# Three of four down batches in seven half-size products, one weight sum made by an accumulating DMA, and an eviction product by product

## The chip, the cores and the metric

The kernel runs on one core of a Trainium2 chip. The metric is device time of one execution in microseconds, the median of several runs.

## What is computed

Two layers of a decoder trunk, 256 tokens of width 2048, float32. Layer 0 mixes tokens by differential attention, layer 1 by a gated recurrence; each is followed by the MLP, the only part that the change touches, and by a gated embedding ("PLE") of the side input p.

```python
def sqrelu_mlp(xn, w_up, w_down):
    return jnp.square(jax.nn.relu(xn @ w_up)) @ w_down

    for i in range(DEPTH):
        ...
        h = h + sqrelu_mlp(rmsnorm(h, g_mlp[i]), w_up[i], w_down[i])
        ...
```

w_up[i] is 2048 x 8192 and w_down[i] 8192 x 2048. The output is the residual stream h (256 x 2048).

## The kernel before

**Float32 on TensorE.** Each float32 operand is split into a high part hi, rounded to TensorE's float32r, and lo = src − hi. ScalarE copies hi (`split`, L356; `split_form`, L464) and VectorE subtracts (L357; L471). A product is then three matmuls: hi·hi, lo·hi and hi·lo, in a seven or plain group in the order of L518, L519 and L521. All weights go through this: a chunk of 512 rows x 512 columns (1 MB) is loaded by SyncE's queue (`load_to`, L457), and a "sub", half of it (256 rows, so 128 partitions x 1024 elements), is split for one step of matmuls.

**Order of the work.** `stream` walks over groups; in each sub it first loads up to two chunks ahead (W_RAW − 1), then splits up to three subs ahead (W_SPLIT − 1), and then writes the sub's matmuls. A scheduler may reorder across engines, so the program's order alone does not fix that of an engine. Raw chunks rotate over three buffers `w_raw` and, every fourth, one in the pool `big`. In the MLP hi/lo pairs rotate over six places: four in the pool `wsp`, one pair of `v4` buffers, one `big` (`split_to`, L481).

**The MLP.** The hidden width is cut into 16 batches of 512. `up(b)` multiplies the weights of batch b by all tokens (8 subs of 16 matmuls, L537), and `up_evict` squares the relu and splits the result. Two ups are followed by a `down` group, over 1024 of the 2048 output columns (`half` 0 or 1) and mostly four batches; per layer: half 1 with batches {0, 1} (the first group), then in turn half 0 and half 1 with {0..3}, {2..5}, {4..7}, ... {12..15}, and at the end half 1 with {14, 15}. So a layer has six full groups, three of each half, one first group of two batches, and the last two groups stand back to back, six batches long.

**Seven products.** A batch of a down group is a 2 x 2 block problem: tokens in two halves, the 512 rows by the parity of their 128-row block, 1024 columns in two chunks. A plain batch takes the eight block products (4 subs of 12 matmuls). A seven batch takes Strassen's seven in Winograd's form (7 subs of 6 matmuls): `FORMS` lists for each its weight operand, its hidden operand and its product P1 to P7, and `SUMS` the weight operands that are sums of blocks (W11, W21 the two row parities of chunk 0, W12, W22 of chunk 1), made by VectorE (L470) one sub ahead. The hidden operand's sums are made in `up_evict` (L810, L814, L815), for j in two halves, so that an up's eviction for a seven batch splits 896 columns where a plain one splits 512. Even batches are seven, odd ones plain (`is_seven`). So the batches of a full group are seven, plain, seven, plain.

**Accumulators and eviction.** All batches of a group add into the same PSUM accumulators, one for each product. P3 and Z (the second token half and chunk of the plain batches) come from the pool `tp`, the others from `acc`. When P1, P5, P6 and P7 are all complete `middle` combines them (one ScalarE copy, L836, L837, twice L839), and at the group's end `evict` adds eight parts to the residual h (L848). At a layer's last groups h goes on to the next norm (`feed`), whose transposes are deferred by one or two subs.

Of the kernel before, what the change touches and what calls it, by code (L numbers as in the profile page):

```python
# [17 lines left out]
P = 128  # L18
# [43 lines left out]
class Group:  # L62
# [41 lines left out]
class Blocks:  # L104


    def __init__(self, w, b, n0):
        r0 = b * BT * P
        rows = w[r0 : r0 + BT * P].rearrange("(c p) n -> p c n", p=P)
        self.chunks = [Chunk(rows[:, :, n0 + i * NB : n0 + (i + 1) * NB], BT) for i in range(2)]  # L110
        for c in self.chunks:
            c.ring = 1
        self.sums = {}

    def of(self, name):
        if name in self.sums:
            return self.sums[name]
        return self.chunks[int(name[2]) - 1].raw[:, int(name[1]) - 1 :: 2]


class SevenGroup:
# [4 lines left out]
    def __init__(self, w, batches, n0, hid, middle, evict):  # L126
        self.hid, self.middle, self.evict, self.subs, self.pre = hid, middle, evict, [], {}
        self.what = []
        for b, seven in batches:
            bl = Blocks(w, b, n0)  # L130
# [11 lines left out]
        self.first, self.last = {}, {}  # L142
        for i, (_, form, nj) in enumerate(self.what):
# [3 lines left out]
        self.mid = max(self.last[k] for k in ("P1", "P5", "P6", "P7"))  # L147
# [27 lines left out]
def trunk_kernel(ctx: ExitStack, tc, a, out):  # L175
# [215 lines left out]
    class Norm(Wide):  # L391
# [35 lines left out]
        def feed(self, nb):  # L427
            self.stat(nb)
            for b in range(2):
                defer(1 + b, lambda b=b: self.transpose(nb, b))  # L430


    def stream(groups):
# [9 lines left out]
        def load_to(i):  # L443
            while done["load"] < min(i + 1, len(chunks)):
# [722 lines left out]
```

## Time and profile before

| | |
|---|---|
| median of 3 runs | 2303.68 us (2303.24 to 2303.95) |
| profiled execution | 2303.79 us, of which the trace spans 2301.9 |
| TensorE (PE) | busy 2277.8 us, 11275 matmuls |
| VectorE (DVE) | busy 1709.6 us, 74% |
| ScalarE (ACT) | busy 1355.5 us, 59% |
| GpSimd (POOL) | busy 47.3 us, 2% |
| mean granted TensorE clock | 1.00 |
| moved by the DMA engines | 434.8 MB, mean 189 GB/s |

Busy time counts stretches in which the engine executes something. Operations of one engine overlap a little, so the mean time of one is somewhat longer than the distance between starts. A line such as L357 is the source line in the kernel before; the line of a helper serves many callers. In the rows `t`, `big`, `v`, `x`, `w_hi`, `w_lo` and `w_raw` are buffers of the pools of those names, `acc` and `tp` PSUM accumulators, and an arrow stands for "written from".

### The profile page before, as it was taken

The page shows a single profiled execution, that of the slowest core. Times are in us where ns is not written, and L with a number is a line of the kernel's source. Part 1 is how long each engine was busy: PE and PEld are TensorE (multiplying, and loading weights), DVE is VectorE, ACT ScalarE, POOL GpSimd, SP SyncE. Part 2 cuts the span into 40 slices and gives each one's busy share as a digit, 9 for nine tenths or more (in the row PEclk, how much of TensorE's full clock was granted, in tenths as well). Part 3 has the DMA queues.
Part 4 walks back from the last instruction along what each step waited for, and adds up shares of the span by engine and source line. Part 5 has one row for each costly group of instructions (what it writes and reads, how often), then busy time and mean ns, then how long its engine had stood idle before and what let it go on. Part 6 is the DMA issues. An engine that isn't in the chain of part 4 may idle for free. (4 is left out here: it accounts for less than half of the span.)

```text
span 2301.9 us, 29004 instructions
## 1 busy us (share of the span) xinstructions
PE 2277.8 (99%) x11275; PEld 1913.4 (83%) x11275; DVE 1709.6 (74%) x2048; ACT 1355.5 (59%) x1836; POOL 47.3 (2%) x79
## 2 busy tenths in 40 slices
PE   8999999999999999999999999999999999999999
PEld 7888888888888888887888887888888888888787
DVE  6676655778878868879666767568887887887974
ACT  6555555655655645646557887555564564564653
POOL 2100000000000000000000000000000000000000
PEclk9999999999999999999999999999999999999999
DMA  7455556456547547545555565645745645745464
GB/s 244 165 185 168 165 171 214 168 182 237 181 162 242 187 161 244 175 162 186 193 190 190 165 201 173 202 157 200 256 151 179 238 167 181 239 167 179 174 210 146
DMA packets 221050, 434.80 MB, mean 189 GB/s; under 512 B 7326, under 2 KB 12064, under 8 KB 220912
## 3 DMA queue, kind: packets, MB, share of 16 engines
q1 hardware_dynamic: 220256, 432.04, 55.5%
q8 instruction: 88, 1.44, 0.3%
q0 software_dynamic: 608, 0.89, 0.2%
q14 instruction: 50, 0.41, 0.1%
q10 hardware_dynamic: 48, 0.02, 0.0%
HBM read 430.82 MB, written 2.10 MB: 188 GB/s over the span
## 5 line engine op out<-in xcount | busy, mean ns | idle before, releaser
L357 DVE TENSOR_TENSOR w_lo<-w_raw,w_hi 128x1024 fp32r<-128x1024 f32 x465 | 564.2, 1221 | 304.5 <-ACT w_hi L356 304.4
L356 ACT CAST w_hi<-w_raw 128x1024 fp32r<-128x1024 f32 x465 | 486.6, 1051 | 419.4 <-PE acc L352 214.9
L537 PE MATMUL acc<-x,w_hi 128*128 128x512 f32 x1368 | 477.3, 396 | 0.0
L350 PE MATMUL acc<-w_hi,x 128*128 128x512 f32 x1152 | 457.1, 397 | 0.0
L351 PE MATMUL acc<-w_lo,x 128*128 128x512 f32 x1152 | 450.4, 391 | 1.9 <-DVE w_lo L357 1.9
L352 PE MATMUL acc<-w_hi,x 128*128 128x512 f32 x1152 | 450.6, 391 | 0.0
L537 PE MATMUL acc<-x,w_lo 128*128 128x256 f32 x1368 | 368.5, 279 | 0.0
L537 PEld LDWEIGHTS acc<-x,w_hi 128*128 128x128 f32 x1368 | 251.9, 188 | 54.7
L537 PEld LDWEIGHTS acc<-x,w_lo 128*128 128x128 f32 x1368 | 257.8, 188 | 7.4
L352 PEld LDWEIGHTS acc<-w_hi,x 128*128 128x128 f32 x1152 | 216.7, 188 | 46.7 <-DVE x L357 0.2
L351 PEld LDWEIGHTS acc<-w_lo,x 128*128 128x128 f32 x1152 | 217.2, 189 | 44.9 <-DVE w_lo L357 3.1
L350 PEld LDWEIGHTS acc<-w_hi,x 128*128 128x128 f32 x1152 | 216.8, 188 | 41.7
L464 ACT CAST w_hi<-t 128x1024 fp32r<-128x1024 f32 x85 | 89.2, 1051 | 128.8 <-PE acc L537 73.9
L537 PE MATMUL acc<-x,big 128*128 128x512 f32 (+1 forms) x688 | 127.7, 338 | 0.0
L356 ACT CAST w_hi<-big 128x1024 fp32r<-128x1024 f32 x87 | 90.7, 1050 | 62.6 <-PE acc L537 26.7
L471 DVE TENSOR_TENSOR w_lo<-t,w_hi 128x1024 fp32r<-128x1024 f32 x85 | 103.8, 1222 | 30.3 <-ACT w_hi L464 30.1
L537 PE MATMUL acc<-x,v 128*128 128x512 f32 (+1 forms) x672 | 124.8, 338 | 0.0
L537 PEld LDWEIGHTS acc<-x,big 128*128 128x128 f32 x688 | 107.9, 188 | 15.5
L537 PEld LDWEIGHTS acc<-x,v 128*128 128x128 f32 x672 | 105.9, 188 | 15.0
L357 DVE TENSOR_TENSOR w_lo<-big,w_hi 128x1024 fp32r<-128x1024 f32 x87 | 105.3, 1218 | 14.1 <-ACT w_hi L356 14.1
L471 DVE TENSOR_TENSOR w_lo<-w_raw,w_hi 128x1024 fp32r<-128x1024 f32 x64 | 78.0, 1219 | 31.9 <-ACT w_hi L464 31.9
L518 PE MATMUL acc<-w_hi,x 128*128 128x512 f32 x256 | 100.3, 392 | 1.4 <-ACT w_hi L464 1.3
(277 smaller groups left out, 3570.0 us busy)
## 6 DMA issues: line engine op xcount, KB each, us to landing
w_raw<-in_w_up_dram SPq DMA_DIRECT2D x96, 1024.0 KB, 5.5
w_raw<-in_w_down_dram SPq DMA_DIRECT2D x96, 1024.0 KB, 5.2
w_raw<-in_w_qkv_dram SPq DMA_DIRECT2D x47, 1024.0 KB, 5.1
big<-in_w_up_dram SPq DMA_DIRECT2D x32, 1024.0 KB, 5.6
big<-in_w_down_dram SPq DMA_DIRECT2D x32, 1024.0 KB, 7.3
w_raw<-in_w_ple_gate_dram SPq DMA_DIRECT2D x32, 1024.0 KB, 5.2
w_raw<-in_w_in_rec_dram SPq DMA_DIRECT2D x32, 1024.0 KB, 5.4
w_raw<-in_w_o_attn_dram SPq DMA_DIRECT2D x16, 1024.0 KB, 5.1
```

Of the source, the lines that this page charges most:

```text
L350: nc.tensor.matmul(ps, lhsT=lh, rhs=rh, start=start, stop=False)
L351: nc.tensor.matmul(ps, lhsT=lh, rhs=rl, start=False, stop=False)
L352: nc.tensor.matmul(ps, lhsT=ll, rhs=rh, start=False, stop=stop)
L356: nc.scalar.copy(hi, src)
L357: nc.vector.tensor_tensor(lo, src, hi.bitcast(F32), op=ALU.subtract)
L464: nc.scalar.copy(s.hi, src)
L471: nc.vector.tensor_tensor(s.lo, src, s.hi.bitcast(F32), op=ALU.subtract)
L518: nc.tensor.matmul(acc[k], lhsT=lh, rhs=rh, start=first, stop=False)
L537: nc.tensor.matmul(o, lhsT=lh, rhs=rh, start=k == 0 and n == 0, stop=k == g.nk - 1 and n == 1)
```

## The change

- Batch b is plain only if b mod 4 is 1. Full groups of half 0 are then seven, plain, seven, seven; those of half 1 seven, seven, seven, plain; the last two groups seven, plain, seven, seven and seven, seven.
- U1 = W11 + W12 is made by a DMA from GpSimd's queue that adds the first half of chunk 0, read once more from DRAM, onto the first half of chunk 1 in SBUF, so W12 alone is no longer there; the other three sums stay on VectorE, T3 in another form. A seven batch's chunks are loaded in two pieces, one for each row parity.
- The products come in another order, P1, P2, P3 first, and each is handed to `done` in the sub after which it is complete: P2, P4, P3 and Z are added to h at once, the combination of P1, P6, P7, P5 as it becomes possible. P4, and P7 where the group has a plain batch, now come from `tp`.
- To make room: the hi/lo places fall from six to five; a fourth buffer of the size of a weight sum (`t4`); batch 3, 7, 11 and 15 keep their operands in two `big` buffers; the transposed p moves to a `big` buffer and is made at the end of each MLP instead of earlier, and the next norm's transposes are deferred further.

In the changed kernel the lines are: lo splits L367 and L482, hi copies L366 and L476, sums L481, loads L467, the accumulate L469, the up's eviction L819 to L828, the combination L862, L867, L871, adds to h L847.

```diff
-    ("W11", X11, "P1"), ("U1", S1, "P5"), ("T2", S2, "P6"), ("T3", S3, "P7"), ("W21", X12, "P2"),
-    ("T4", X22, "P4"), ("W22", S4, "P3"),
+    ("W11", X11, "P1"), ("W21", X12, "P2"), ("W22", S4, "P3"), ("U1", S1, "P5"), ("T2", S2, "P6"),
+    ("T3", S3, "P7"), ("T4", X22, "P4"),
 )
-SUMS = {"U1": ("W11", "W12"), "T2": ("U1", "W22"), "T4": ("T2", "W21"), "T3": ("W12", "W22")}
+SUMS = {"T2": ("U1", "W22", ALU.add), "T3": ("T2", "W11", ALU.subtract), "T4": ("T2", "W21", ALU.add)}
...
-        self.chunks = [Chunk(rows[:, :, n0 + i * NB : n0 + (i + 1) * NB], BT) for i in range(2)]
-        for c in self.chunks:
+        cols = [rows[:, :, n0 + i * NB : n0 + (i + 1) * NB] for i in range(2)]
+        self.chunks = [Chunk(c, BT) for c in cols]
+        for i, c in enumerate(self.chunks):
             c.ring = 1
+            if seven:
+                half = lambda raw, i: raw[:, i * SK : (i + 1) * SK]
+                c.pieces = [(lambda raw, i=i: half(raw, i), cols[c is self.chunks[1]][:, i::2]) for i in range(2)]
+        if seven:
+            self.chunks[1].more = (lambda raw: raw[:, :SK], cols[0][:, 0::2])
...
+        self.aside = ("P4", "P7") if len(self.subs) % len(FORMS) else ("P4",)
...
-        return wk.tile(shape, dtype, tag="t4", name="t4", bufs=3)
+        return wk.tile(shape, dtype, tag="t4", name="t4", bufs=4)
...
+                if c.more is not None:
+                    nc.gpsimd.dma_start(c.more[0](c.raw), c.more[1], accum_op=ALU.add)
...
-                    at = turn["split"] % (W_SPLIT + 2) if s.chunk.ring else 2
-                    if at == 0:
+                    if s.chunk.ring and turn["split"] % (W_SPLIT + 1) == 0:
                         s.hi, s.lo = (v4([P, SK, NB], F32R) for _ in range(2))
-                    elif at == 1:
-                        both = big([P, 2, SK, NB], F32R)
-                        s.hi, s.lo = both[:, 0], both[:, 1]
...
-                    if i == g.mid:
-                        g.middle(acc)
+                    for k in acc:
+                        if g.last[k] == i:
+                            g.done(k, acc)
...
+    ALONE = {"P2": (0, 0), "P4": (1, 0), "P3": (0, 1), "Z": (1, 1)}
...
-        return b % 2 == 0
+        return b % SLOTS != 1
...
+            if at == 3:
+                return Batch(True, big([P, 2, 7, P], F32R), big([P, 2, 7, P], F32R))
...
+            def done(k, acc):
+
+                have.add(k)
+                if k in ALONE:
+                    add(*ALONE[k], acc[k])
+                if k == "P1":
+                    c1 = t4([P, 2, NB])
+                    keep["P1"], keep["M"] = c1[:, 0], c1[:, 1]
+                    nc.scalar.copy(keep["P1"], acc["P1"])
+                if "A" not in have and {"P1", "P6"} <= have:
+                    have.add("A")
+                    nc.vector.tensor_tensor(keep["M"], keep["P1"], acc["P6"], op=ALU.subtract)
...
             def evict(acc):
...
+                for q, at in (("P1", (0, 0)), ("B", (1, 0)), ("M", (0, 1)), ("N", (1, 1))):
+                    add(*at, keep[q])
                 if bs[-1] == NBT - 1:
                     for n in range(2):
-                        norm_out().feed(2 * half + n)
+                        norm_out().feed(2 * half + n, 2 + 2 * n if half else 4 + 3 * n)
+                    if half == 0:
+                        defer(7, lambda: p_setup(l))
```

Three places show how the order of the instructions moves. The first is VectorE's queue at the start of a full group of half 0 (batches 4 to 7), around the up's eviction (`t_4401` and `t_4412`, with the change `t_5874` and `t_5888`, are the halves of the hidden operand). Before:

```order
L471 TENSOR_TENSOR w_lo<-t_4381,w_hi 128x1024
L471 TENSOR_TENSOR v_4439<-w_raw,v_4438 128x1024
L806 TENSOR_TENSOR t_4401<-acc,t_4402 128x2x128
L806 TENSOR_TENSOR t_4401<-acc,t_4405 128x256
L806 TENSOR_TENSOR t_4412<-acc,t_4413 128x2x128
L806 TENSOR_TENSOR t_4412<-acc,t_4416 128x256
L357 TENSOR_TENSOR big<-t_4401,big 128x512
L357 TENSOR_TENSOR big<-t_4412,big 128x512
L471 TENSOR_TENSOR big<-t_4441,big 128x1024
L471 TENSOR_TENSOR w_lo<-w_raw,w_hi 128x1024
L357 TENSOR_TENSOR w_lo<-w_raw,w_hi 128x1024 x2
L357 TENSOR_TENSOR w_lo<-big,w_hi 128x1024
```

and with the change:

```order
L481 TENSOR_TENSOR t_5920<-t_5907,w_raw 128x1024
L827 TENSOR_TENSOR t_5874<-t_5874 128x128
L823 TENSOR_TENSOR t_5888<-t_5888 128x256
L828 TENSOR_TENSOR t_5874<-t_5874 128x128
L827 TENSOR_TENSOR t_5888<-t_5888 128x128
L482 TENSOR_TENSOR v_5918<-t_5907,v_5917 128x1024
L367 TENSOR_TENSOR big<-t_5874,big 128x896
L828 TENSOR_TENSOR t_5888<-t_5888 128x128
L481 TENSOR_TENSOR t_5935<-t_5907,w_raw 128x1024
L367 TENSOR_TENSOR big<-t_5888,big 128x896
L482 TENSOR_TENSOR w_lo<-t_5920,w_hi 128x1024
L482 TENSOR_TENSOR w_lo<-t_5935,w_hi 128x1024
```

The four adds of the up (L806) were followed by two 512-column splits and the remaining lo splits of the first subs. Now the four adds (L819), the sum T2 (`t_5907`) and one of the hidden operand's sums stand just ahead of the rows shown; the sums T3 (`t_5920`) and T4 (`t_5935`), the hidden operand's other sums and two 896-column splits follow, with T2's lo (`v_5918`) among them, and the lo splits of T3 and T4 come last.

The second is SyncE's queue of loads around the group of half 1 with batches 2 to 5, with the numbers of the buffers. Before:

```order
L457 DMA w_raw_5135<-in_w_down_dram 128x4x512
L457 DMA w_raw_5216<-in_w_down_dram 128x4x512
L457 DMA big_5147<-in_w_down_dram 128x4x512
L457 DMA w_raw_5237<-in_w_down_dram 128x4x512
L457 DMA w_raw_5291<-in_w_down_dram 128x4x512
L457 DMA big_5303<-in_w_down_dram 128x4x512
```

and with the change:

```order
L467 DMA w_raw_5160<-in_w_down_dram 128x2x512 x2
L467 DMA w_raw_5250<-in_w_down_dram 128x2x512 x2
L467 DMA w_raw_5277<-in_w_down_dram 128x2x512 x2
L467 DMA big_5189<-in_w_down_dram 128x2x512 x2
L467 DMA big_5361<-in_w_down_dram 128x4x512
L467 DMA w_raw_5333<-in_w_down_dram 128x4x512
```

`big_5189` is the second chunk of the group's second batch (the numbers give the order in which buffers were asked for): it stands behind `w_raw_5250` and `w_raw_5277`, both chunks of the third. GpSimd's queue has its three accumulates of this group onto `w_raw_5093`, `w_raw_5277` and `big_5189`, in this order.

The third is VectorE's queue at the end of the group of half 0. Before:

```order
L357 TENSOR_TENSOR v_4680<-w_raw,v_4679 128x1024
L357 TENSOR_TENSOR big<-w_raw,big 128x1024
L357 TENSOR_TENSOR w_lo<-w_raw,w_hi 128x1024
L848 SCALAR_TENSOR_TENSOR h<-acc,n_r_3440,h 128x512 x2
L848 SCALAR_TENSOR_TENSOR h<-t_4624,n_r_3440,h 128x512
L848 SCALAR_TENSOR_TENSOR h<-t_4625,n_r_3440,h 128x512
L357 TENSOR_TENSOR w_lo<-w_raw,w_hi 128x1024 x2
L357 TENSOR_TENSOR big<-big 128x1024
L848 SCALAR_TENSOR_TENSOR h<-tp,n_r_3440,h 128x512 x2
L848 SCALAR_TENSOR_TENSOR h<-t_4624,n_r_3440,h 128x512
L848 SCALAR_TENSOR_TENSOR h<-t_4625,n_r_3440,h 128x512
L357 TENSOR_TENSOR w_lo<-w_raw,w_hi 128x1024
```

and with the change:

```order
L862 TENSOR_TENSOR t_6159<-t_6159,acc 128x512
L367 TENSOR_TENSOR w_lo<-w_raw,w_hi 128x1024
L867 TENSOR_TENSOR t_6220<-tp,t_6159 128x512
L367 TENSOR_TENSOR w_lo<-w_raw,w_hi 128x1024
L871 SCALAR_TENSOR_TENSOR t_6159<-acc,t_6159 128x512
L871 SCALAR_TENSOR_TENSOR t_6220<-acc,t_6220 128x512
L847 SCALAR_TENSOR_TENSOR h<-tp,n_r_3430,h 128x512
L847 SCALAR_TENSOR_TENSOR h<-t_6159,n_r_3430,h 128x512
L847 SCALAR_TENSOR_TENSOR h<-t_6220,n_r_3430,h 128x512
L847 SCALAR_TENSOR_TENSOR h<-t_6159,n_r_3430,h 128x512
L847 SCALAR_TENSOR_TENSOR h<-t_6220,n_r_3430,h 128x512
L367 TENSOR_TENSOR w_lo<-w_raw,w_hi 128x1024
```

The eight adds to h (L848), which stood in two groups of four, are spread now (L847: five here, three ahead of the rows shown), and the combination (L862, L867, L871), which was in the middle of the group, stands between the first splits of the next up.

## Rows read from the trace of the kernel before

**Rows 1.** The page: busy time of each engine, and TensorE's granted clock in 40 slices.
```profile
PE 2277.8 (99%) x11275; PEld 1913.4 (83%) x11275; DVE 1709.6 (74%) x2048; ACT 1355.5 (59%) x1836; POOL 47.3 (2%) x79
PEclk9999999999999999999999999999999999999999
```

**Rows 2.** Windows: a first group, a half-0 group, an up, two last groups; sums.
```profile
core 0: us, PE busy (x) PEld busy (x) DVE busy (x) ACT busy (x) POOL busy (x), PEclk, DMA share, GB/s
448.10:468.70 20.60, 20.60 (x92) 16.89 (x91) 18.60 (x24) 15.36 (x20) 0.00 (x0) 1.00 0.90 299
513.70:554.70 41.00, 41.00 (x182) 33.75 (x181) 37.73 (x40) 27.99 (x32) 0.00 (x0) 1.00 0.76 260
642.30:687.00 44.70, 44.70 (x257) 38.98 (x256) 30.50 (x37) 21.40 (x28) 0.00 (x0) 1.00 0.41 138
1032.50:1098.40 65.90, 64.17 (x287) 51.98 (x286) 60.86 (x70) 42.01 (x57) 0.00 (x0) 1.00 0.55 190
2131.20:2197.30 66.10, 64.47 (x287) 51.86 (x286) 61.60 (x71) 41.11 (x57) 0.00 (x0) 1.00 0.56 192
...
sum 124.80, PE 123.47 PEld 101.20 DVE 114.72 ACT 82.58 POOL 0.00; mean PE 41.16 PEld 33.73 DVE 38.24 ACT 27.52 POOL 0.00
...
sum 124.80, PE 123.47 PEld 101.19 DVE 114.80 ACT 82.89 POOL 0.00; mean PE 41.16 PEld 33.73 DVE 38.27 ACT 27.63 POOL 0.00
```

**Rows 3.** TensorE's timeline: start, length, engine, line, operands, count, [idle before <- releaser].
```profile
513.66 0.39 PE L518 MATMUL acc<-w_hi,x 128*128 128x512 f32 x1
...
515.02 0.39 PE L518 MATMUL acc<-w_hi,x 128*128 128x512 f32 x1
...
605.20 0.51 PE L518 MATMUL acc<-big,x 128*128 128x512 f32 x1 [1.33 <-ACT big L464]
```

**Rows 4.** VectorE's timeline of the half-0 group that starts at 513.7.
```profile
513.07 1.61 DVE L806 TENSOR_TENSOR t<-acc,t 128x256 f32<-128x256 f32 x4
516.94 1.29 DVE L357 TENSOR_TENSOR big<-t,big 128x512 fp32r<-128x512 f32 x2 [2.25 <-ACT big L356]
...
534.46 1.22 DVE L471 TENSOR_TENSOR w_lo<-w_raw,w_hi 128x1024 fp32r<-128x1024 f32 x1
...
537.87 1.22 DVE L357 TENSOR_TENSOR w_lo<-w_raw,w_hi 128x1024 fp32r<-128x1024 f32 x1
...
542.47 1.28 DVE L839 SCALAR_TENSOR_TENSOR t<-acc,t 128x512 f32<-128x512 f32 x2
543.67 1.21 DVE L357 TENSOR_TENSOR w_lo<-big,w_hi 128x1024 fp32r<-128x1024 f32 x1
...
548.99 1.41 DVE L848 SCALAR_TENSOR_TENSOR h<-acc,n_r,h 128x512 f32<-128x512 f32 x2 [0.70 <-PE acc L521]
550.32 1.40 DVE L848 SCALAR_TENSOR_TENSOR h<-t,n_r,h 128x512 f32<-128x512 f32 x2
```

**Rows 5.** VectorE's groups by shape: busy us, mean ns of one | idle before.
```profile
L357 DVE TENSOR_TENSOR x<-t,x 128x896 fp32r<-128x896 f32 x32 | 33.5, 1083 | 0.5 <-ACT x L356 0.5
...
L357 DVE TENSOR_TENSOR big<-t,big 128x512 fp32r<-128x512 f32 x32 | 20.8, 688 | 25.0 <-ACT big L356 25.0
...
L810 DVE TENSOR_TENSOR t<-t 128x256 f32<-128x256 f32 x32 | 12.7, 419 | 0.2
...
L814 DVE TENSOR_TENSOR t<-t 128x128 f32<-128x128 f32 x32 | 7.9, 284 | 0.0
```

**Rows 6.** DMA issues: count, KB each, median us from issue to landing.
```profile
big<-in_w_down_dram SPq DMA_DIRECT2D x32, 1024.0 KB, 7.3
...
w_raw<-in_w_ple_proj_dram SPq DMA_DIRECT2D x8, 512.0 KB, 3.7
...
t<-in_p_dram POOLq DMA_DIRECT2D x2, 256.0 KB, 3.2
```

**Rows 7.** GpSimd's line L559 (loads of p): duration ns min/median/max.
```profile
L559 POOL DMA_DIRECT2D t<-in_p_dram x2: 778/789/800, 132.7 to 1179.8; - x2
```

**Rows 8.** SyncE's timeline: issues of two loads.
```profile
513.18 0.37 SPq L457 DMA_DIRECT2D w_raw<-in_w_down_dram  x1
513.60 1.07 SPq L457 DMA_DIRECT2D big<-in_w_down_dram  x1
```

More of the change, by code (lines that the diff above doesn't have):

```diff
@@ L43 @@
 class Chunk:
-    ring = 0
+    ring, more = 0, None
     def __init__(self, src, nk):
@@ L117, in of, with __init__ @@
             return self.sums[name]
[L118 removed]
+        n, k = {"W11": (0, 0), "W21": (0, 1), "U1": (1, 0), "W22": (1, 1)}[name]
+        return self.chunks[n].raw[:, k * SK : (k + 1) * SK]
 class SevenGroup:
     flip = False
[L126 to L127 removed]
+    def __init__(self, w, batches, n0, hid, done, evict):
+        self.hid, self.done, self.evict, self.subs, self.pre = hid, done, evict, [], {}
         self.what = []
         for b, seven in batches:
[L130 removed]
+            bl = Blocks(w, b, n0, seven)
             if seven:
@@ L466, in split_form @@
             if after in SUMS:
-                load_to(cidx[id(bl.chunks[1])])
-                one, two = (bl.of(nm) for nm in SUMS[after])
+                one, two, op = SUMS[after]
                 bl.sums[after] = t4([P, SK, NB])
-                nc.vector.tensor_tensor(bl.sums[after], one, two, op=ALU.add)
+                nc.vector.tensor_tensor(bl.sums[after], bl.of(one), bl.of(two), op=op)
             nc.vector.tensor_tensor(s.lo, src, s.hi.bitcast(F32), op=ALU.subtract)
@@ L559, in p_setup @@
         nc.gpsimd.dma_start(p_sb, p[l, 0].rearrange("(t q) d -> q t d", q=P))
-        pT[l] = Operand(*(wk.tile([P, 2, SEQ], F32R, name="pT" + c, bufs=1) for c in "hl"))
+        both = big([P, 2, 2, SEQ], F32R)
+        pT[l] = Operand(both[:, 0], both[:, 1])
         def transpose():
@@ L843, in evict @@
-            def evict(acc):
-                r2 = norm_in().r2
-                for t, n, ps, other in ((0, 0, "P2", "P1"), (1, 0, "P4", "B"), (0, 1, "P3", "M"), (1, 1, "Z", "N")):
-                    hb = h[:, t, hs[n]]
-                    for part in (acc[ps], keep[other]):
-                        nc.vector.scalar_tensor_tensor(
-                            hb, in0=part, scalar=r2[:, t : t + 1], in1=hb, op0=ALU.mult, op1=ALU.add
-                        )
+            keep, have = {}, set()
@@ new lines, in add @@
+            def add(t, n, part):
+                hb = h[:, t, hs[n]]
+                nc.vector.scalar_tensor_tensor(
+                    hb, in0=part, scalar=norm_in().r2[:, t : t + 1], in1=hb, op0=ALU.mult, op1=ALU.add
+                )
+            def done(k, acc):
[9 more added lines that the diff above has]
+                    nc.vector.tensor_tensor(keep["M"], keep["P1"], acc["P6"], op=ALU.subtract)
+                if "B" not in have and {"A", "P7"} <= have:
+                    have.add("B")
+                    cb = t4([P, 2, NB])
+                    keep["B"], keep["N"] = cb[:, 0], cb[:, 1]
+                    nc.vector.tensor_tensor(keep["B"], acc["P7"], keep["M"], op=ALU.add)
+                if "M" not in have and {"B", "P5"} <= have:
+                    have.add("M")
+                    for q, o in (("M", "M"), ("N", "B")):
+                        nc.vector.scalar_tensor_tensor(
+                            keep[q], in0=acc["P5"], scalar=-1.0, in1=keep[o], op0=ALU.mult, op1=ALU.subtract
+                        )
@@ L857, in mlp @@
+            groups.append(SevenGroup(a["w_down"][l], [(b, is_seven(b)) for b in bs], n0, hid, done, evict))
         for b in range(0, NBT, 2):
```

27 lines of the change are left out of this document (6 added, 21 removed).

## The prediction

> **What bounds the kernel now.** I read the profile's page first, for the engines' shares: TensorE (PE) is busy 2277.8 us of a span of 2301.9 us and its clock row is all nines [rows 1], so nothing outside TensorE can give back more than 24.1 us, and only fewer matmuls or less waiting help. The next engine is VectorE (DVE) at 74%, but that is a mean over unlike stages, so the second view is the windows by stage [rows 2]. In an up stretch DVE has 30.5 us of work in 44.7. In a full down group of four batches it has 38.2 us in a mean of 41.6 (each half's three groups take 124.8 together), and in the last group 60.9 in 65.9. Down is thus the place where DVE is within a tenth of TensorE, and that is where the change works. The third view is TensorE's timeline [rows 3]: a step of six 512-column matmuls of a seven-product batch begins at 513.66, the next at 515.02, so 0.227 us a matmul; and at 605.20 it stands idle 1.33 us for a split that ScalarE (ACT) made late. The fourth is DVE's timeline of the first full group [rows 4]: operations on 1024 columns follow each other every 1.137 us ((537.87 − 534.46)/3), though one is shown as 1.22, because they overlap.
>
> **The matmuls removed.** A batch in seven products is 42 matmuls, a plain one 48. A full group goes from two plain batches to one, 180 to 174, and the last (six batches, one plain instead of three) from 270 to 258; the first is unchanged. Per layer 6 × 6 + 12 = 48, in both layers 96; with 41.0 us/180 = 0.228 each this is **−21.9 us** on the engine that sets the end, if nothing is waited for. TensorE alone would need 39.7 us for a full group and 58.8 for the last.
>
> **The DVE work added.** Before, a seven-product batch costs DVE seven lo splits and four sums, a plain one four splits: 11 + 4 + 11 + 4 = 30 operations a full group. After, U1 comes from the accumulating DMA, so 10 + 10 + 10 + 4 = 34; the last group goes from 45 to 54. At 1.137 that is +4.5 us a full group and +10.2 in the last. So 38.2 becomes 42.8, over the 39.7 that TensorE needs, and DVE becomes the bound of these groups. Where batch 3, 7, 11 or 15 was plain, its eviction now makes seven operands: two 896-column splits (1.083) for two of 512 (0.688), and in each of two halves one 256-column and two 128-column sums (0.42 + 2 × 0.28) [rows 5]: +2.8 us. Of this DVE can hide what the light up stretches take. How much that is depends on the deadlines, since splits run only three steps (3 × 1.37 us) ahead; I counted them out for both kinds of full group, from T0, the end of the matmuls of the up before it (513.66 in rows 3).
>
> *Half 0 (seven, plain, seven, seven).* The up's four adds end at T0 + 1.0 (513.07 + 1.61 [rows 4]). Then the order puts the sums T2, T3 and T4, two 896-column splits and the small sums before the lo of T2 and of T3: 5 × 1.137 + 2 × 1.0 + 1.5 = 9.2, so T3's lo is there at 10.1. TensorE wants it in its sixth step, in the last third: 5 × 1.37 + 0.9 = 7.7. Stall 2.3. At the far end, four splits of the next up stand between and behind the adds of the last products: from the last lo 4 × 1.137 + 4 × 0.60 + 5 × 0.66 = 10.2 (0.60 and 0.66 as half of 543.67 − 542.47, and of 550.32 − 548.99 [rows 4]), where the up wants its fourth split after 0.5 + 3 × 2.8 = 8.9: another 1.2. So 39.7 + 2.3 + 1.2 = 43.2, and 3 × 43.2 − 124.8 = **+4.8 a layer**.
>
> *Half 1 (seven, seven, seven, plain).* DVE cannot go on splitting until ACT has done relu, square and the copies of the up before: it idles 2.25 us [rows 4], and its next lo starts at about T0 + 5.3. From there to the last lo of the third batch's T4 are 23 operations, 26.1 us, so 31.4; wanted at 20 × 1.37 + 0.9 = 28.3. Stall 3.1. The order also issues the second batch's second chunk behind both of the third's on SP's queue, and the first of these waits for a buffer that the first batch's U1 leaves free; so the load starts near T0 − 0.6 and lands 7.3 us later [rows 6]. Behind it comes the accumulate, **an operation this trace does not have**. Its nearest rows: 512 KB by SP land after 3.7 us [rows 6] and GpSimd's (POOL's) issue takes 0.79 [rows 7], so 4.5; 1 MB in the buffers concerned 7.3, so 8.1; 256 KB from POOL 3.2 [rows 6]. A gain is excluded, since it starts only when the load is there. I take 5, nearest the 512 KB row: 6.7 + 5 = 11.7, wanted at 11.0, so 0.6 late; at 8.1 it is 3.7 late. So 39.7 + 3.1 + 0.6 = 43.4, and 3 × 43.4 − 124.8 = **+5.4 a layer**. The Trainium skill (DMA: Bandwidth & Descriptors, "Anatomy of one DMA — SWDGE (gpsimd) path") fits a POOL-issued transfer by 2.0 us plus the bytes at 436 GB/s: an estimate of 3.2 us for 512 KB, by which the 0.6 would go and the sum be 2340; no run here shows it for an accumulate.
>
> *Last group.* 60.9 + 10.2 + 2.6 (one eviction, shortened by its overlap) = 73.7 us of DVE work, plus the ACT gap of about 2: 75.7 against 65.9, **+9.8 a layer**. The first group has 18.6 of DVE in 20.6 and the same matmuls: nothing.
>
> **The rest.** The products' adds are the same 12 operations, done earlier or later: nothing beyond the deadlines above. The split ring falls from six to five entries and three are ahead at a time, so two are left; if that cover went, one split (1.14) a step would show. SP issues two 512 KB pieces for each 1 MB; an issue takes 0.37 to 1.07 us [rows 8], and 14 of them stand in a full group's 40 us. The accumulates add 0.5 MB a batch: a full group moves 10.7 MB (260 GB/s in 41.0), then some 12.2, 305 GB/s at TensorE's pace, where the first group ran at 299 with the DMA engines 90% busy; the up's 0.41 takes the rest [rows 2]. The move of the p transposes adds one 512-column split beside the last half-1 pair: 0.6 at most. A fourth buffer of the sums' kind may shorten stalls elsewhere, within the 24.1 us of rows 1.
>
> **Sum.** 4.8 + 5.4 + 9.8 = 20.0 a layer, 40 in all (the second layer runs as the first: its last group takes 66.1 [rows 2]). The profiled execution took 2303.79, 0.1 from the median 2303.68: **2344 us**. Own range 2322 (each of these stalls half as long) to 2363 (the accumulate at 8.1, 6 × 3.1).
>
> **Rivals.**
> *The accumulate is the wait (slower).* If it lands 10 us after its issue, or queues behind the loads that make the DMA engines 90% busy, U1 of the second batch in half 1 is some 5 to 6 us late instead of 0.6: six groups, +30 to 35, 2375 to 2380. For it: it reads and writes what it adds to, and loads in the large buffers took 7.3 instead of 5. Against: it waits on a queue of its own, with 256 KB landing in 3.2. 0.17.
> *POOL is held up by DVE (slower).* POOL's two issues of 256 KB in this trace took 0.78 to 0.80 us [rows 7]. If each accumulate waited out one DVE operation of 1.22 before its issue, the six groups would lose 1.2 each: 2351. The Trainium skill (SBUF — State Buffer, "Who interferes with whom") has DVE operations with two operands in SBUF contend with GpSimd's reads, and infers that the generation of descriptors, a write, stays free of it; by that there is no such wait, and the two issues agree. 0.05.
> *DVE's holes close (faster).* If the scheduler's order leaves DVE no hole, because T2's lo fills the ACT gap and the early adds lie in stretches in which DVE waits, the groups take 39.8 (half 0), 39.7 (half 1) and 72.7 (last): 3 × 39.8 + 3 × 39.7 − 249.6 = −11.1, and +6.8 in the last, −4.3 a layer, **2295**. It decides at one point: the first batch's T3 lo must be ready by T0 + 7.7, and the second batch's first lo start by T0 + 2.5. For it: DVE did idle 2.25 there, and the mean of 42.8 a group leans on up stretches with 14 us free. Against: the order printed puts T2 to T4 and the wide splits ahead of that lo. 0.12.
> *Gain and loss cancel.* Stalls of half of what I count in the full groups, and last groups no longer than before, since the splits of the pair behind them shift: 2344 − 21.6 − 19.6 = 2303. 0.07.
>
> **How the numbers follow.** Forecast 0.59, its neighbours as above. Faster 0.12, same 0.07 (a measurement of this kernel can tell about 0.2%, 4.6 us, from no change), slower 0.81. The range leaves out the fastest rival, and reaches from 2310, somewhat under the forecast's own lower end for last groups below 70, to beyond the late accumulate, 2385.
>
> **What would show it.** Down windows of 43 to 44 us in place of 41 to 42.7 and last groups near 75, with about 174 and 258 matmuls; DVE busy 42 us or more in the full ones; TensorE waiting for lo splits in the first batch of half 0 and in the third of half 1, 2 to 3 us a group; idle of DVE before U1's split ended by an accumulate of about 5 us. The granted clock stays at 1.00. I am wrong if full groups come in at 40 with little waiting (DVE's holes), if TensorE's largest wait is for U1 (the accumulate), or if the loads land later throughout (the DMA engines).

## The result and the profile after

The changed kernel takes **2393.18 us** (median of 4, 2387.79 to 2394.25) against 2303.61: a ratio of 1.0384, 95% interval 1.0366 to 1.0402. It is slower, as forecast, but by 89.6 us instead of 40, and outside the range.

The page's first part has 96 matmuls fewer, as counted, and yet more TensorE time and 97.0 us of idle time where there were 24.1 [rows 1]:

```profile
PE 2293.5 (96%) x11179; PEld 1904.0 (80%) x11179; DVE 1797.8 (75%) x2158; ACT 1410.2 (59%) x1884; POOL 104.7 (4%) x127
```

The windows of the changed kernel (columns as in [rows 2]): a first group, a full group of half 0, one of half 1, an up stretch (two ups), and both layers' last groups.

```profile
447.90:469.00 21.10, 20.82 (x91) 16.71 (x90) 19.56 (x24) 15.60 (x20) 0.00 (x0) 1.00 0.86 299
513.40:562.20 48.80, 43.72 (x177) 34.97 (x176) 42.35 (x47) 29.58 (x33) 2.38 (x2) 0.93 0.75 237
607.60:652.30 44.70, 41.07 (x175) 32.11 (x174) 39.62 (x41) 29.60 (x34) 2.38 (x2) 1.00 0.79 244
652.30:696.70 44.40, 44.40 (x257) 38.81 (x257) 30.31 (x37) 22.09 (x29) 1.20 (x1) 1.00 0.49 154
1064.40:1147.40 83.00, 67.98 (x282) 52.71 (x280) 75.54 (x87) 49.32 (x64) 5.52 (x5) 0.94 0.60 174
2207.50:2286.00 78.50, 68.12 (x283) 51.82 (x282) 75.70 (x87) 49.66 (x64) 5.52 (x5) 0.96 0.62 184
```

The half-0 group takes 48.8 (forecast 43.2, with 1.2 of it in the up behind), the half-1 group 44.7 (43.4), the last ones 83.0 and 78.5 (75.7). Not all groups of a kind are alike: the six of half 0 take 45.0 to 50.8, those of half 1 43.8 to 46.1. Two things the forecast did not have: in some groups the granted clock is below 1, and the up stretch takes 44.4 where it took 44.7 [rows 2].

The waits of VectorE (engine, line and what it waited for; us in total, times, longest) name the new one: T2's sum, VectorE's first reader of U1, waits for the accumulate.

```profile
DVE t L481 <- DMA big<-in_w_down_dram: 44.2, 12, 6.0
DVE t L481 <- DMA w_raw<-in_w_down_dram: 35.3, 15, 3.6
```

One such wait in full, third batch of the half-0 group that starts at 513.4. SyncE's timeline, then GpSimd's, then VectorE's, then TensorE's:

```profile
529.43 0.97 SPq L467 DMA_DIRECT2D big<-in_w_down_dram  x2
535.11 0.37 SPq L467 DMA_DIRECT2D w_raw<-in_w_up_dram  x1
535.66 0.37 SPq L467 DMA_DIRECT2D big<-in_w_up_dram  x1
```

```profile
536.62 1.21 POOL L469 DMA_DIRECT2D big<-in_w_down_dram  x1 [9.36 <-DVE t L481]
```

```profile
539.07 1.21 DVE L482 TENSOR_TENSOR v<-t,v 128x1024 fp32r<-128x1024 f32 x1
546.32 1.23 DVE L481 TENSOR_TENSOR t<-big 128x1024 f32<-128x1024 f32 x1 [6.04 <-DMA big<-in_w_down_dram]
547.46 1.22 DVE L482 TENSOR_TENSOR w_lo<-t,w_hi 128x1024 fp32r<-128x1024 f32 x1
548.60 2.35 DVE L482 TENSOR_TENSOR w_lo<-w_raw,w_hi 128x1024 fp32r<-128x1024 f32 x2
550.87 1.22 DVE L482 TENSOR_TENSOR w_lo<-big,w_hi 128x1024 fp32r<-128x1024 f32 x1
```

```profile
544.30 0.39 PE L526 MATMUL tp<-w_hi,x 128*128 128x512 f32 x1
548.74 1.22 PE L528 MATMUL tp<-w_lo,x 128*128 128x512 f32 x2 [4.04 <-DVE w_lo L482]
549.75 0.63 PE L525 MATMUL acc<-w_hi,big 128*128 128x512 f32 x1
550.18 0.63 PE L526 MATMUL acc<-w_hi,big 128*128 128x512 f32 x1
```

The load is issued 16 us into the group and lands after some 7 us; only then is the accumulate issued, with two loads of the next up just ahead of it; VectorE's sum goes on at 546.3. And the sum stands *ahead* in VectorE's queue: the splits behind it (L482 at 547.46 to 550.87, the previous batch's T4 and this batch's W11, W21 and W22) need no accumulate, but wait too, and TensorE is waiting for the first of them. After the stall the matmuls start 0.43 us apart instead of 0.227. Windows around it show the clock: 1.00 up to the stall, 0.51 behind it, then 1.00 again.

```profile
538.00:544.00 6.00, 6.00 (x28) 4.99 (x27) 2.28 (x3) 3.90 (x4) 0.00 (x0) 1.00 1.05 314
544.00:548.00 4.00, 0.69 (x4) 0.23 (x2) 1.68 (x2) 1.04 (x1) 0.00 (x0) 1.00 1.03 330
548.00:555.00 7.00, 6.26 (x15) 4.97 (x16) 7.00 (x7) 2.19 (x3) 0.00 (x0) 0.51 0.12 28
555.00:562.00 7.00, 7.00 (x33) 5.76 (x32) 6.59 (x8) 5.03 (x6) 0.00 (x0) 1.00 0.82 277
```

So TensorE, idle for most of 4 us, ran about 7 us at 1.2 instead of 2.4 GHz: another 3.4 us (an estimate, 7.00 × 0.49, and an upper one, since VectorE was busy all of these 7 us too).

In half 1 the accumulate is late in the place that the forecast looked at, the second batch. GpSimd's, VectorE's and TensorE's timelines of the group that starts at 607.6:

```profile
614.76 1.19 POOL L469 DMA_DIRECT2D big<-in_w_down_dram  x1 [1.90 <-DMA big<-in_w_down_dram]
621.98 1.23 DVE L481 TENSOR_TENSOR t<-big 128x1024 f32<-128x1024 f32 x1 [3.00 <-DMA big<-in_w_down_dram]
623.15 0.50 PE L525 MATMUL acc<-v,big 128*128 128x512 f32 x1 [1.81 <-ACT v L476]
```

GpSimd's line of the accumulates has the price that the forecast had to guess: 1.2 us to issue, and a median of 7.0 us from issue to landing.

```profile
L469 POOL DMA_DIRECT2D w_raw<-in_w_down_dram x32: 1177/1197/1280, 429.7 to 2243.1; - x32
...
DMA to landing us min/median/max: 5.6/7.0/10.7
```

### The profile page after: what moved, and what is told of

Its sections match the earlier page's. It is cut to its first block, busy times and chain, and to the rows that moved or that the text cites. A ratio compares the mean times of both kernels' runs of the same rounds, so it can differ in the third digit from the quotient of the medians.

```text
span 2390.5 us, 29312 instructions
## 1 busy us (share of the span) xinstructions
PE 2293.5 (96%) x11179; PEld 1904.0 (80%) x11179; DVE 1797.8 (75%) x2158; ACT 1410.2 (59%) x1884; POOL 104.7 (4%) x127
## 5 line engine op out<-in xcount | busy, mean ns | idle before, releaser
L367 DVE TENSOR_TENSOR w_lo<-w_raw,w_hi 128x1024 fp32r<-128x1024 f32 x477 | 578.5, 1221 | 296.5 <-ACT w_hi L366 296.3
L366 ACT CAST w_hi<-w_raw 128x1024 fp32r<-128x1024 f32 x477 | 497.3, 1050 | 393.6 <-PE acc L362 214.6
L545 PE MATMUL acc<-x,w_hi 128*128 128x512 f32 x1648 | 572.1, 394 | 0.0
L360 PE MATMUL acc<-w_hi,x 128*128 128x512 f32 x1152 | 457.3, 398 | 0.0
L362 PE MATMUL acc<-w_hi,x 128*128 128x512 f32 x1152 | 450.7, 391 | 0.0
L545 PE MATMUL acc<-x,w_lo 128*128 128x256 f32 x1648 | 442.1, 279 | 4.9 <-DVE w_lo L367 4.9
L545 PEld LDWEIGHTS acc<-x,w_hi 128*128 128x128 f32 x1648 | 303.9, 188 | 63.8
L545 PEld LDWEIGHTS acc<-x,w_lo 128*128 128x128 f32 x1648 | 309.9, 188 | 15.9 <-DVE w_lo L367 7.2
L476 ACT CAST w_hi<-w_raw 128x1024 fp32r<-128x1024 f32 x126 | 129.9, 1050 | 116.1 <-PE acc L545 79.8
L482 DVE TENSOR_TENSOR w_lo<-w_raw,w_hi 128x1024 fp32r<-128x1024 f32 x126 | 151.6, 1219 | 50.5 <-ACT w_hi L476 50.5
L476 ACT CAST w_hi<-t 128x1024 fp32r<-128x1024 f32 x115 | 120.0, 1047 | 65.4 <-DVE t L481 53.6
L482 DVE TENSOR_TENSOR w_lo<-t,w_hi 128x1024 fp32r<-128x1024 f32 x115 | 139.3, 1217 | 8.1 <-ACT w_hi L476 8.1
L525 PE MATMUL acc<-w_hi,big 128*128 128x512 f32 x286 | 116.4, 407 | 9.8 <-ACT w_hi L476 9.8
L481 DVE TENSOR_TENSOR t<-t,w_raw 128x1024 f32<-128x1024 f32 x96 | 116.6, 1217 | 0.0
L526 PE MATMUL acc<-w_hi,big 128*128 128x512 f32 x286 | 115.7, 404 | 0.0
L366 ACT CAST w_hi<-big 128x1024 fp32r<-128x1024 f32 x77 | 79.9, 1050 | 59.7 <-PE acc L545 55.7
```

Source lines behind the costliest of these rows:

```text
L360: nc.tensor.matmul(ps, lhsT=lh, rhs=rh, start=start, stop=False)
L362: nc.tensor.matmul(ps, lhsT=ll, rhs=rh, start=False, stop=stop)
L366: nc.scalar.copy(hi, src)
L367: nc.vector.tensor_tensor(lo, src, hi.bitcast(F32), op=ALU.subtract)
L476: nc.scalar.copy(s.hi, src)
L481: nc.vector.tensor_tensor(bl.sums[after], bl.of(one), bl.of(two), op=op)
```

## The experiments

Several experiments change the order of VectorE's queue: "in turn" says that T2's sum is queued behind the lo split of the sub before U1, an order and not a wait. Theory A: accumulates that land late make the long stalls, and with them the clock's fall. Theory B, the forecast's own: VectorE's extra operations are the bound. Theory C: VectorE's holes close. Medians in us, and ratios to the kernel before with their intervals:

| run | median | ratio |
|---|---|---|
| changed kernel | 2393.2 | 1.0384 [1.0366, 1.0402] |
| e1, no accumulate | 2329.6 | 1.0114 [1.0099, 1.0129] |
| e2, U1 by VectorE | 2366.4 | 1.0268 [1.0253, 1.0284] |
| e3, plain copy | 2351.2 | 1.0209 [1.0192, 1.0226] |
| e6, T2's sum in turn | 2372.7 | 1.0303 [1.0289, 1.0317] |
| e8, as e6, four raw buffers | 2390.7 | 1.0376 [1.0362, 1.0390] |
| e9, as e1, no T3 sum | 2290.0 | 0.9938 [0.9924, 0.9951] |
| e4, even batches | 2312.4 | 1.0037 [1.0024, 1.0050] |
| e5, even, in turn | 2304.2 | 1.0003 [0.9994, 1.0012] |
| e7, even, U1 by VectorE | 2304.6 | 1.0004 [0.9995, 1.0013] |
| e10, even, four raw buffers | 2356.5 | 1.0229 [1.0215, 1.0243] |
| e11, as e10, in turn | 2307.0 | 1.0014 [1.0005, 1.0023] |
| e13, as e11, `v4` moved | 2297.1 | 0.9973 [0.9963, 0.9983] |
| e14, as e13, U1 by VectorE | 2298.5 | 0.9980 [0.9971, 0.9988] |
| e12, before, `v4` moved | 2293.9 | 0.9958 [0.9946, 0.9971] |
| e15, as e12, relu queued later | 2294.4 | 0.9960 [0.9946, 0.9974] |

### The accumulate taken away or made a copy, and VectorE's load raised and lowered

e1, against the changed kernel:

```diff
-        if seven:
-            self.chunks[1].more = (lambda raw: raw[:, :SK], cols[0][:, 0::2])
```

> The changed kernel without the accumulating DMA: the products that should use W11 + W12 use W12 alone, so that part of the computation is left out; all else is as changed. Theory A (the late accumulates make the long stalls, and each long stall also halves TensorE's clock for some 7 us after it): the waits of VectorE for a load before T2's sum (79.5 us) go, the granted clock is 1.00 in all down groups, and the time falls by 50 us or more, to 2320 to 2345. Theory B (VectorE's extra work is the bound, as forecast, and the accumulate only sits in its slack): the time falls by less than 20 us and stays over 2370. Theory C (VectorE's holes close once nothing waits for a load): full groups of 39.8 us, 2295.

63.5 us went, as theory A says: the accumulates cost that much. The same 11179 matmuls take 24.2 us less of TensorE's busy time, and its idle time falls by 39.4, from 97.0 us to 57.6:

```profile
PE 2269.3 (98%) x11179; PEld 1891.8 (81%) x11179; DVE 1796.8 (77%) x2158; ACT 1410.3 (61%) x1884; POOL 48.2 (2%) x79
```

The mean granted clock rose from 0.988 (of 2390.5 us, so 28.7 us lost) to 0.998 (4.7 of 2326.9). So about 24 of the 63.5 are the clock's: an estimate, with which the busy time agrees. What stays is theory B's: a half-0 group, the up stretch behind it, a half-1 group and the first layer's last groups are

```profile
513.30:554.90 41.60, 40.55 (x178) 32.91 (x177) 41.60 (x46) 29.68 (x33) 0.00 (x0) 1.00 0.73 248
554.90:600.80 45.90, 44.56 (x255) 38.71 (x254) 36.91 (x46) 22.81 (x30) 0.00 (x0) 1.00 0.50 166
600.80:642.50 41.70, 40.56 (x176) 32.28 (x175) 39.62 (x42) 29.50 (x34) 0.00 (x0) 1.00 0.65 227
1034.00:1109.50 75.50, 66.11 (x283) 51.87 (x281) 75.48 (x87) 49.48 (x64) 0.80 (x1) 0.95 0.50 164
```

VectorE is busy 41.60 of 41.60 us in the first and 75.48 of 75.50 in the last. With the 1.5 us by which the up is longer than 44.4, half 0 takes 43.1 (forecast 43.2); half 1 41.7 (forecast 42.8 without its 0.6 for the accumulate); the last groups 75.5 (75.7). The forecast had TensorE wait for lo splits. Most of its waits in e1's down groups are one step removed, for ScalarE's hi copy of a sum that VectorE made late:

```profile
PE tp L523 <- ACT w_hi L474: 17.1, 20, 2.4
```

e2, on top of e1:

```diff
-SUMS = {"T2": ("U1", "W22", ALU.add), ...
+SUMS = {"U1": ("W11", "W12", ALU.add), "T2": ("U1", "W22", ALU.add), ...
```

> The changed kernel with U1 summed by VectorE as before, so no accumulating DMA, and one more operation of 1.137 us on VectorE for each seven batch (3 in a full group, 5 in the last). Theory A alone, with slack on VectorE: as the run without the sum, within 10 us. If VectorE is the bound of the down groups once the accumulate is gone: 2 x (6 x 3.4 + 5.7) = 52 us over the run without the sum. Theory B: over 2393, since it only adds to VectorE.

36.8 us over e1 for 48 operations (the expectation's 46 leave out the two first groups), 0.77 us each of the 1.137. That lies between the 10 and the 52 expected: VectorE is the bound of most of these stretches, with a little room. e9 takes as many away from e1:

```diff
-SUMS = {"T2": ..., "T3": ("T2", "W11", ALU.subtract), "T4": ...}
+SUMS = {"T2": ..., "T4": ...}
```

> The kernel without the accumulate (2329.6) and without T3's sum too: the seventh product takes W11 in its place, so those two sums are left out. It takes 46 operations of 1.137 us (52 us) from VectorE's down groups. Adding as many (U1's sum on VectorE) cost 36.8. If VectorE is the bound of these groups without the accumulate, the time falls by 20 to 37 us, to 2293 to 2310, with full groups at 39.7 to 40.5 and last groups near 68. If what is left of the loss is something else (the order of the products, the eviction, ScalarE), it falls by less than 10.

39.6 us under e1, a little more than expected; the groups shown have TensorE without waits in both halves, and VectorE still nearly full in the last groups:

```profile
512.80:552.30 39.50, 39.50 (x175) 32.62 (x174) 39.35 (x45) 29.83 (x33) 0.00 (x0) 1.00 0.76 259
597.30:637.10 39.80, 39.80 (x176) 32.39 (x175) 37.72 (x40) 29.18 (x34) 0.00 (x0) 1.00 0.77 264
1019.50:1091.30 71.80, 65.25 (x282) 51.51 (x280) 70.00 (x82) 48.98 (x64) 0.80 (x1) 0.98 0.50 167
```

The same number of operations added or removed moves the time by nearly the same amount: theory B is shown for what is left without the accumulate.

e3 keeps the transfer and drops the addition:

```diff
-                    nc.gpsimd.dma_start(c.more[0](c.raw), c.more[1], accum_op=ALU.add)
+                    nc.gpsimd.dma_start(c.more[0](c.raw), c.more[1])
```

> The changed kernel with the accumulate replaced by a plain DMA of the same 512 KB from the same queue to the same place (the products that should use W11 + W12 use W11 alone: the addition is left out). If the addition in the DMA is what is slow, the median landing falls from 7.0 us to about 4.5 (3.7 for 512 KB by SyncE's queue and 0.8 of issue) and the time falls by 20 us or more. If the transfer is late because it starts only after the load it adds to, and shares the DMA engines with the loads issued behind, the landing stays at 6 to 10 us and the time within 10 us of 2393.

The first reading holds: the landing falls to 4.4, about as expected, and the time by 42.0 us:

```profile
DMA to landing us min/median/max: 3.9/4.4/8.7
```

But 21.5 us over e1 stay. They belong to the transfer itself, which starts only behind the load and adds 0.5 MB a batch; e3 does not separate the two. The addition in the DMA makes each transfer 1.7 us longer at the least (5.6 against 3.9) and 2.6 in the median, and that is worth the 42.0. A part of it is the issue: 1.18 to 1.28 us for the accumulate, 0.72 to 0.80 for the plain copy.

### The place of T2's sum in VectorE's queue

e4, against the changed kernel, and e5 to it:

```diff
-        return b % SLOTS != 1
+        return b % 2 == 0
```

```diff
+                with tc.issue_after(state["lo"]):
-                nc.vector.tensor_tensor(bl.sums[after], bl.of(one), bl.of(two), op=op)
+                    nc.vector.tensor_tensor(bl.sums[after], bl.of(one), bl.of(two), op=op)
```

> The changed kernel with the old choice of batches (even ones in seven products, odd ones plain): 180 matmuls a full group as before, ten VectorE operations for a seven batch instead of eleven, two accumulates a full group instead of three. Theory A: the accumulate has a whole plain batch of time (11 us more) for the second seven batch of a group, so stalls stay below 2 us a group, and the time is within 15 us of 2304. Theory B: VectorE has 28 operations a full group instead of 30, so 2300 to 2304. If the eviction product by product or the smaller ring costs by itself, 2310 or more with short waits spread over all groups.

> As the run with even batches in seven products and accumulates, but T2's sum is queued on VectorE behind the lo split of the sub before U1 (order alone, no wait added). In that run nearly all full groups took 40.80 us, but three took 7.9, 8.2 and 8.5 longer, and there T2's sum, which waits for the accumulate, stood ahead of the plain batch's lo splits on VectorE. If the place in the queue made these stalls, they go and the time is 2312.4 - 24.6 = 2288. If the accumulate itself is too late there, the stalls stay and so does 2312.

e4 lost 8.6 us although TensorE has the old work and VectorE less. The timeline of VectorE at one of the three long stalls: T2's sum of the second seven batch stands ahead of the plain batch's splits (L367 at 869.77), which it holds back 7.2 us.

```profile
859.63 1.23 DVE L482 TENSOR_TENSOR w_lo<-t,w_hi 128x1024 fp32r<-128x1024 f32 x1 [0.16 <-ACT w_hi L476]
868.02 1.23 DVE L481 TENSOR_TENSOR t<-w_raw 128x1024 f32<-128x1024 f32 x1 [7.17 <-DMA w_raw<-in_w_down_dram]
869.17 0.68 DVE L367 TENSOR_TENSOR big<-t,big 128x512 fp32r<-128x512 f32 x1
869.77 2.35 DVE L367 TENSOR_TENSOR w_lo<-w_raw,w_hi 128x1024 fp32r<-128x1024 f32 x2
```

In e5 the three long stalls are gone, but only 8.2 of the 24.6 us came back, since the waits spread over other groups (41.4 to 43.3 instead of 40.8). The forecast of 2288 was a miss.

> The changed kernel with the same edit: T2's sum queued behind the lo split of the sub before U1. If the place in VectorE's queue made most of the loss, the long stalls of half 0 (4 to 5.6 us and the half clock behind each) go: 2345 or less. If the accumulates land after TensorE wants U1 (they land 26 to 33 us after a group's start in half 0, where U1 of the third batch is wanted at about 26), the stalls only move from the splits ahead to U1's own: 2370 to 2393.

e6, the same edit on the changed kernel, gained 20.5 of the 63.5 us: the stalls mostly moved to U1's own splits, as its second reading had it. The queue's order is a part of the loss, the lateness the larger one.

> Even batches in seven products, U1 summed by VectorE, no accumulating DMA: what is left of the change is the order of the products, the eviction product by product and the buffers. If these parts gain by themselves (groups of 40.80 and ups of 44.40 instead of 41.0 to 42.7 and 44.7 to 45.0), 2285 to 2297, within 5 us of the run with accumulates in turn. If the one operation more on VectorE for each batch matters (30 a full group, as before), 2300 to 2306.

e7 equals e5 and the kernel before: the products' order, the eviction product by product and the buffers together give no gain, and the accumulate none at two seven batches a group. That is not to say that each of these parts is worth nothing: the buffers' new places gain, as e12 shows below, and e7 is 10.7 us slower than e12, which has the old order of the work and `v4` at a fast place as e7 has. So the rest of the reorganization loses about what the places gain.

### Loads earlier

```diff
-W_RAW = 3
+W_RAW = 4
```

with the room from one `t4`, one `t2` and one `t1` buffer.

> The changed kernel with T2's sum in turn and one raw buffer more (four and the one in `big`, so that loads run three chunks ahead; the room comes from one buffer each of the sums, of 2 KB and of 1 KB). If the accumulates are late because their loads wait for a buffer, they now start up to a chunk's time (5 us) earlier, VectorE's waits for them (44.7 us with T2's sum in turn) fall below 20 and the time to 2340 to 2355, toward the 2330 of the run without accumulates. If they are late because they are slow among other loads, or the smaller buffers cost as much, 2365 to 2385.

> Even batches in seven products with accumulates (2312.4 before), with the additional raw buffer and no order forced. If the loads' start is what makes the accumulate late: stalls of 8 us in three groups go, 2285 to 2295, under the kernel before. If the place of T2's sum in VectorE's queue matters more, 2305 to 2315.

> The same with T2's sum in turn (2304.2 with three raw buffers). With loads earlier and the sum in turn neither cause is left: 2283 to 2293, groups of 40.80 throughout and last groups near 66. If the smaller buffers cost elsewhere, 2295 to 2305.

e8 (with T2's sum in turn) missed, and does not settle how much the loads' start costs with three seven batches: VectorE's waits for accumulates fell from 44.7 to 22.0 us, but TensorE's waits for ScalarE's copies rose to

```profile
PE tp L527 <- ACT w_hi L476: 35.9, 26, 2.5
PE acc L527 <- ACT v L476: 13.4, 7, 4.6
```

and the buffers taken away may be the reason. The new buffer layout of e8, e10 and e11 also puts `v4` at a slow place, which e13 below prices at 9.9 us. e10, with every kind of load earlier, is 44 us slower than e4, and most of that hangs on the order: e11 has the same loads and the same places, the sum in turn, and is 49.5 us faster. Their waits of VectorE for accumulates, e10's first:

```profile
DVE t L481 <- DMA w_raw<-in_w_down_dram: 41.8, 13, 9.1
```

```profile
DVE t L482 <- DMA w_raw<-in_w_down_dram: 2.4, 1, 2.4
```

With loads earlier *and* the sum in turn, next to nothing waits for an accumulate. Yet e11 was no faster than before: its ups take 44.9 again, its full groups 41.1 to 41.8.

### The place of two buffers

e12, against the kernel before (e13 the same to e11, e14 with U1 by VectorE):

```diff
+    vp = ctx.enter_context(tc.tile_pool(name="vp", bufs=2))
     wk = ctx.enter_context(tc.tile_pool(name="wk", bufs=2))
...
-        return wk.tile(shape, dtype, tag="v4", name="v4", bufs=2)
+        return vp.tile(shape, dtype, tag="v4", name="v4", bufs=2)
```

> The kernel before with nothing but the two `v4` buffers moved in SBUF (a pool of their own, allocated earlier: byte 159520 of a partition instead of 218080, 32 instead of 224 beyond a multiple of 256). In the kernel before, a matmul whose moving operand lies in `v4` takes 233 ns, in `w_hi` 227; in the changed kernel, where `v4` lies 64 bytes further on, both take 227. If the place is the cause: 227 ns, ups of 44.4 to 44.7 and 2294 to 2300. If it is the order of the work around them: 233 ns and 2304 still.

> Even batches in seven products with accumulates, T2's sum in turn, four raw buffers (2307.0, where nothing waits for an accumulate any more, but full groups take 41.1 to 41.4 and ups 44.9), with `v4` moved as above. If the place is the cause of these: groups of 40.8, ups of 44.4 and 2307 - 12 x 0.4 - 14 x 0.5 = 2295. If not: 2307.

> The same with U1 summed by VectorE and no accumulating DMA. If an accumulate that comes in time is worth the one operation of 1.137 us that it takes from VectorE for each batch: slower than the run with accumulates by up to 2 x 17 x 1.1 = 37 us where VectorE is the bound, so over 2300. If VectorE has room at two seven batches a group: the same within 3 us, so that the accumulate gives nothing there.

The place is the cause. (The new pool also shifts the work buffers that stood ahead of `v4`, all by 8192 bytes; `w_hi` stays where it was.) In the kernel before, the matmuls on `v` of one sub start 0.2325 us apart ((520.03 − 519.10)/4), against 0.227 for `w_hi` [rows 3]:

```profile
519.10 0.39 PE L518 MATMUL acc<-v,x 128*128 128x512 f32 x1
...
520.03 0.63 PE L521 MATMUL acc<-v,x 128*128 128x512 f32 x2
```

in e12 0.225 ((519.26 − 518.36)/4):

```profile
518.36 0.39 PE L519 MATMUL acc<-v,x 128*128 128x512 f32 x1
...
519.26 0.62 PE L522 MATMUL acc<-v,x 128*128 128x512 f32 x2
```

and its up stretches take 44.40, as this window of e12 has it:

```profile
553.70:598.10 44.40, 44.40 (x257) 38.80 (x256) 30.44 (x37) 20.21 (x27) 0.00 (x0) 1.00 0.41 140
```

2293.9 is 9.7 us under the kernel before, for a move of two buffers. The change had moved `v4` by 64 bytes as a by-product; its 14 up stretches between down groups gained 6.5 us by it, while its down groups have VectorE as their bound. e13 gains 9.9 over e11, and e14 is 1.4 over e13, with intervals that overlap: an accumulate in time is worth next to nothing at two seven batches a group. No run that computes the whole result is faster than e12, which has nothing of the change but the place.

e15 was to remove the stalls that e12 keeps:

```diff
+                    with tc.issue_after(state["hi"]):
-                    nc.scalar.activation(x, x, AF.Relu)
+                        nc.scalar.activation(x, x, AF.Relu)
```

> The kernel before with `v4` moved (2293.9), and the relu of an up's eviction queued on ScalarE behind the last hi copy written so far. In six full groups TensorE still stands 1.1 to 1.4 us for a hi copy that ScalarE's queue has behind the relu, square and copies of the up before it; these groups take 42.5 instead of 40.8. If the place in the queue is the cause, the six groups take 40.8 and the time is 2293.9 - 6 x 1.7 = 2284. If the relu then holds back the eviction and VectorE's splits, the same 2294 or more.

It changed nothing: its trace has the same hi copy behind the relu, since that copy is written later than those the relu was queued behind. So it says nothing of the cause.

## Why the prediction was wrong

The windows of three traces, summed by stage over both layers, give the change against the kernel before. To half 0 belongs the delay of the up stretch behind each group, which is what that lasts beyond 44.4 us. What lies outside the rows moves by 0.3 us at most.

| us | forecast without the accumulate | e1, no accumulate | changed kernel |
|---|---|---|---|
| two first groups | 0 | +1.9 | +1.7 |
| six groups of half 0, with the delay | +9.6 | +9.8 | +43.9 |
| six groups of half 1 | +7.2 | +0.9 | +20.1 |
| two last groups | +19.6 | +19.2 | +29.5 |
| 14 up stretches, delay apart | 0 | −6.5 | −6.5 |
| the whole span | +36.4 | +25.0 | +88.6 |

The lines behind its second row, the sums over the six half-0 groups of the changed kernel and of e1 (249.6 before, [rows 2] for one layer):

```profile
sum 287.80, PE 256.75 PEld 203.09 DVE 253.82 ACT 177.69 POOL 14.30; mean PE 42.79 PEld 33.85 DVE 42.30 ACT 29.61 POOL 2.38
sum 251.40, PE 242.80 PEld 196.63 DVE 250.66 ACT 177.66 POOL 0.00; mean PE 40.47 PEld 32.77 DVE 41.78 ACT 29.61 POOL 0.00
```

- **The matmuls removed** came out as a count: 96 fewer. What they are worth alone no run measures.
- **The DVE work added** came out in half 0 and in the last groups, within 0.4 us. Half 1 was 6.3 us too dear in all (1.1 a group): VectorE has 39.6 us of work in the group shown, not 42.8. The place of `v4` gave 6.5 us in the up stretches, which the forecast could not have. So the whole without the accumulate, 2340, was 10 us over the 2329.6 of e1.
- **The accumulate is the step that failed**: 63.5 us instead of 3.6. By the table 34.1 of them fall in half 0 and 10.3 in the last groups, where the forecast had no term for it, and 19.2 in half 1, where it had 3.6. Three things were wrong. Its *size*: "I take 5"; measured 5.6 to 10.7, median 7.0, issue 1.2 instead of 0.79. The lower bound of 4.5 was under the fastest, the upper one of 8.1 was passed; of the rows given, the 7.3 of the 1 MB loads into the large buffers [rows 6] came closest, not the 512 KB one. Its *place*: it was priced in half 1 alone. There the mechanism is the forecast one (614.76 + 7.20 = 621.96, 14.4 after T0 where 11.7 was forecast; TensorE runs on to 13.7 after T0, not 11.0, and then stands 1.81 us for U1). In half 0 the third batch's accumulate landed some 33 us after T0. And the *queue*: the forecast followed which load stands behind which on SyncE's queue, but did not ask what stands behind T2's sum on VectorE's.
- "The granted clock stays at 1.00" was wrong: about 24 of those 63.5 us are the clock's, which fell behind the long stalls.
- **The rival "the accumulate is the wait"** had the mechanism and the 10 us, at a chance of 0.17 and a price of 30 to 35 us, because it too counted six groups of half 1 only. Of the 63.5, the plain transfer makes 21.5 and the addition 42.0 (e3).
- **"POOL is held up by DVE"** fell: all 48 issues took 1.18 to 1.28 us, in full down groups and in the light ups alike, and the plain copies of e3, issued in the same places, 0.72 to 0.80. The Trainium skill (SBUF — State Buffer, "Who interferes with whom") infers that descriptor generation stays free of VectorE's operations with two operands in SBUF. The trace agrees: 1.18 to 1.28 us wherever VectorE is busy or not. The other citation of the Trainium skill (DMA: Bandwidth & Descriptors, "Anatomy of one DMA — SWDGE (gpsimd) path") gave an estimate of 3.2 us for 512 KB; the plain copy's fastest took 3.9, the accumulate's 5.6: that fit has no term for the addition, and the measurement decides.
- **"DVE's holes close"** fell: without the accumulate full groups take 41.5 to 42.8 (e1), not 39.8, and reach about that only with VectorE's work reduced (e9).

## What to carry to other kernels

An operation that moves work from a busy engine to a DMA is priced from its landing back to the event that lets it start, for every place where it occurs, and then by what stands behind its first reader on that reader's queue: here the scheduler put that reader ahead of work that was due and ready. A stall can cost more than its length: the one of 4.0 us shown made its group and the up stretch behind it 6.7 us longer than in e1 (513.4 to 607.6, against 513.3 to 600.8), with the clock at one half for a while behind it. And before a half-per-cent gain or loss is explained by the work, look whether the buffers moved.

## What the runs showed of the hardware that was not expected

- A matmul of 512 columns takes 227 or about 233 ns with the same shape, clock and order of work, by where its moving operand lies: slow at byte 218080 of a partition (the kernel before), fast at 218144 (the changed kernel) and at 159520 (e12). Why is open; only these places and those of e11 (219104, slow) and e13 (167712, fast) were seen. All slow ones lie 224 bytes beyond a multiple of 256, all fast ones 32.
- Up stretches sped up with it (44.99 or 44.70 to 44.40), though there `v4` holds the stationary operand.
- An accumulating DMA of 512 KB into SBUF takes 5.6 to 10.7 us from issue to landing; the one shown, beside two loads of the next up, took 9.7. A plain copy of the same bytes from the same queue takes 3.9 to 8.7. How much of the spread is the traffic beside it was not tested.
- The issue alone takes GpSimd 1.18 to 1.28 us for the accumulate and 0.72 to 0.80 for the plain copy.
- The granted clock was 0.51 for about 7 us behind TensorE's idle time of 4 us, and 1.00 again behind that.
